# Decoder step on one core: nine more feed-forward slices as seven block products, and an activation table load given a fixed place

## The chip, the core and the metric

The kernel runs on 1 core of one Trainium2 chip. Its time is device time in microseconds, the median over runs. A core has five engines that run their own instruction queues and wait for each other by semaphores: TensorE (PE: matmuls, with weight loads shown apart as PEld), VectorE (DVE), ScalarE (ACT), GpSimd (POOL) and SyncE (SP, which here only issues DMAs). DMAs run on 16 engines that all queues share. Matmuls accumulate in PSUM, eight banks of 512 float32 a partition; all else lies in SBUF.

## The reference

A two-layer decoder step for 1024 prompt tokens and 8 sample tokens, model width 1024. Each layer has a mixer (layer 0: a gated recurrence, layer 1: stick-breaking attention; both in parallel with attention into 256 memory tokens) and a SwiGLU feed-forward network with inner width 2816. RMSNorm stands around every sub-layer. The part that the change touches is

```
def swiglu(h, w_gu, w_down):
    gate, up = jnp.split(h @ w_gu, 2, axis=-1)
    return (jax.nn.silu(gate) * up) @ w_down
...
    h = h + rmsnorm(swiglu(rmsnorm(h, g[2]), w_gu[l], w_down[l]), g[3])
```

with w_gu of 1024 x 5632 and w_down of 2816 x 1024 per layer.

## The kernel before, in words

Tokens are cut into two groups, g = 0 with 512 prompt tokens and g = 1 with 512 prompt and the 8 sample tokens (520 columns, handled as two halves of 260). Activations lie transposed, features on the partitions. A float32 product is made of three reduced-precision ones: activations and weights are split into a high and a low part (`split_to`, `split_w`), and high x high, high x low and low x high are summed in PSUM.

**Plain slices.** The feed-forward network is worked through in 22 slices of 128 inner columns, grouped into five parts (`PARTS`: 5, 5, 4, 4 and 4 slices). For each slice `ffn.part` makes gate and up with `proj` (line 269), each 8 blocks x 3 products x 2 halves, so 96 matmuls of 260 columns for g = 1; the gate goes through `silu` (Exp, Ln, Exp on ACT), and the product is split for the down projection. After a part's slices come 8 down columns, added into the float32 result R by DVE. A slice of weights is four loads of 256 KB (`split_w`): SP issues the load into a `wraw` tile, ACT copies the high part to a `wspl` tile, DVE subtracts for the low part. PSUM is a pool `mmp` of two double banks, a pool `smp` of three and one of one bank.

**Block-product slices.** Layer 1's second group is computed last, by `ffn_w`. There the gate/up product of a slice is seen as a 2 x 2 by 2 x 2 block product and made from seven block products (`gate_up_w`, line 526) of 4 x 3 = 12 matmuls each, 84 in all. The operands are sums of weight blocks and sums of activation blocks. The weight sums lie in DRAM: `weight_sums` (line 590) issues eight DMAs for each part on POOL's queue, half of them copies and half of them accumulating into their target, each behind a mark that POOL executes when a given value is there. In the kernel before, ACT copies that value into a small tile first (line 604). The activation sums are made by `sums_w` (line 329) on DVE and ACT during the first, plain slices (`gate_up_q`, which uses ACT's Silu instead of Exp, Ln, Exp). A block slice loads seven pieces of 256 KB, four of them from the sums.

The block slices use four PSUM tiles q0 to q3 (`Q`), in a pool `quads` with two buffers of each, opened after `mmp`, `smp` and `nsp` are closed (lines 1441 and 1442). Within a slice the tiles are chained: pb starts as -pa (L561), pc as -pb (L564), pd is copied out (L570), and L572 to L578 form gate times up.

**Order.** The program is traced in the order that `weave` gives: it takes steps from several generators in proportion to the weights written beside them. A scheduler then places each engine's instructions by that order and by its own costs, taking one that is ready ahead of one that is not. `tc.issue_after(ins)` ties the instructions of its block that run on the engine of `ins` behind `ins`; on other engines it orders nothing. The stage with layer 0's second group reads

```
    weave((chain(b0.sb(), b0.mem()), 30), (chain(f1.part(0), f1.part(1)), 18), (islice(ws, 16), 17))
    weave((chain(f1.part(2), f1.part(3), f1.part(4)), 24), (ws, 24))
```

where `ws` are the weight sums for layer 1: 16 of them beside parts 0 and 1, 24 beside parts 2 to 4. In the last stage `ffn_w(1, o1.x, 4)` has four plain slices and 18 block slices. Its end, `finish_rows` (line 749), sums squares on PE, takes Ln and Exp on ACT and forms the output rows on DVE. `nc.scalar.preload_act_table_set` (line 661) names the table set that holds both Ln and Exp; it has no operand, so nothing but the trace order places it.

## Time and profile before

| | |
|---|---|
| median of 3 runs | 2532.29 us (2530.27 to 2533.87) |
| the profiled execution | 2531.92 us, span 2530.2 us |
| TensorE clock granted, mean | 0.997 |
| matmuls | 15437 |
| block slices: matmuls under L554 | 864 + 648 |
| HBM read and written | 325.73 and 75.94 MB |

The span runs from the first to the last instruction on the core. A row of the timeline gives start, length, engine, line, operation, output and input tiles, shape and count; neighbours of one kind are merged, and the bracket names the idle time before and what ended it. A row of waits gives the waiting instruction, what released it, the total, the number of times and the longest. A row of stretches gives the stretch, its length, busy time and number of instructions of PE, PEld, DVE, ACT and POOL, then the granted clock, the share of time in which the 16 DMA engines worked, and GB/s. A queue's row gives packets, MB and the share of 16 engines' time; a DMA group's row the number of transfers, their size and the median time from issue to landing.

### The profile page before, as it was taken

Reading aid. Unit: us, or ns where it says so; the run is one execution under the profiler, and the core shown is the slowest. Engines: PE = TensorE matmul, PEld = TensorE weight load, DVE = VectorE, ACT = ScalarE, POOL = GpSimd, SP = SyncE. Lnnn points to the kernel's source line nnn. Section 1 sums busy time; section 2 is a strip of 40 time slices with the busy share of each in tenths; the row PEclk is TensorE's granted clock in tenths of the full one; section 3 lists DMA queues with packets and bytes.
Section 4 is the critical chain, followed back from the end, with each engine's and each line's share of the span. In section 5 each row is a group of like instructions: output and inputs, shape, how many; then the busy total and the mean of one; then the engine's idle time right before and its main releaser. Section 6 shows DMA issues by size and latency. Waiting matters only on the chain. (4 is left out here: it accounts for less than half of the span.)

```text
span 2530.2 us, 40541 instructions
## 1 busy us (share of the span) xinstructions
PE 2499.1 (99%) x15437; PEld 2169.2 (86%) x15437; DVE 1572.9 (62%) x2811; ACT 1199.7 (47%) x2294; POOL 91.5 (4%) x139
## 2 busy tenths in 40 slices
PE   8999999999999999999999999999999999999998
PEld 6888888877877888999999989876676797999997
DVE  6666556654765576655444585667577648855665
ACT  6346543243433454555333454555454445554444
POOL 1000000000000000000111100011000000000000
PEclk9999999999999999999999999999999999999998
DMA  6352242233644446476778866444343334365542
GB/s 186 111 163 67 71 154 80 63 107 117 180 125 129 129 146 190 145 179 168 182 198 212 245 186 191 152 147 118 112 146 117 97 114 122 121 188 145 150 139 68
DMA packets 502221, 358.20 MB, mean 142 GB/s; under 512 B 19077, under 2 KB 451794, under 8 KB 502026
## 3 DMA queue, kind: packets, MB, share of 16 engines
q1 hardware_dynamic: 483466, 301.08, 39.8%
q0 software_dynamic: 18560, 54.53, 8.9%
q8 instruction: 121, 1.98, 0.3%
q14 instruction: 74, 0.61, 0.1%
HBM read 325.73 MB, written 75.94 MB: 159 GB/s over the span
## 5 line engine op out<-in xcount | busy, mean ns | idle before, releaser
L277 PE MATMUL mm<-x,ws 128*128 128x260 f32 (+1 forms) x7968 | 1421.9, 334 | 0.8 <-ACT x L401 0.8
L277 PEld LDWEIGHTS mm<-x,ws 128*128 128x128 f32 x7968 | 1191.1, 188 | 173.4 <-issue 23.5
L263 ACT CAST ws<-w 128x512 fp32r<-128x512 f32 x728 | 430.7, 592 | 747.3 <-PE mm L277 610.5
L264 DVE TENSOR_TENSOR ws<-w,ws 128x512 fp32r<-128x512 f32 x728 | 474.3, 655 | 310.7 <-ACT ws L263 294.4
L277 PE MATMUL mm<-m,ws 128*128 128x512 f32 (+1 forms) x2112 | 414.3, 347 | 0.0
L277 PEld LDWEIGHTS mm<-m,ws 128*128 128x128 f32 x2112 | 325.8, 188 | 54.6 <-issue 9.5
L669 PE MATMUL q<-m,ws 128*128 128x260 f32 x1056 | 128.8, 283 | 0.0
L669 PEld LDWEIGHTS q<-m,ws 128*128 128x128 f32 x1056 | 127.2, 188 | 0.4 <-ACT hT L487 0.2
L545 DVE TENSOR_TENSOR ws<-w,ws 128x512 fp32r<-128x512 f32 x126 | 86.5, 691 | 59.9 <-ACT ws L544 56.2
L554 PE MATMUL q<-y,ws 128*128 128x260 f32 x864 | 113.0, 283 | 0.0
L544 ACT CAST ws<-w 128x512 fp32r<-128x512 f32 x126 | 77.9, 621 | 67.7 <-PE q L669 26.9
L294 DVE TENSOR_SCALAR t<-mm 128x512 f32<-128x512 f32 (+1 forms) x82 | 56.8, 693 | 82.6 <-PE mm L277 82.3
L554 PEld LDWEIGHTS q<-y,ws 128*128 128x128 f32 x864 | 107.6, 188 | 0.0
L449 DVE TENSOR_TENSOR r<-r,mm 128x512 f32<-128x512 f32 (+1 forms) x96 | 66.1, 689 | 62.4 <-PE mm L277 61.5
L705 DVE TENSOR_TENSOR t<-t,mm 128x512 f32<-128x512 f32 (+1 forms) x66 | 45.6, 690 | 85.9 <-PE mm L277 85.9
L298 DVE TENSOR_TENSOR t<-t,t 128x512 f32<-128x512 f32 (+1 forms) x66 | 45.8, 694 | 68.1 <-ACT t L297 68.1
L554 PE MATMUL q<-x,ws 128*128 128x260 f32 x648 | 86.3, 282 | 0.0
L554 PEld LDWEIGHTS q<-x,ws 128*128 128x128 f32 x648 | 81.3, 188 | 0.0
L317 DVE TENSOR_TENSOR st<-st,n 128x512 f32<-128x512 f32 (+1 forms) x98 | 67.3, 694 | 6.6 <-ACT n L316 5.0
L285 DVE TENSOR_TENSOR m<-t,m 128x512 fp32r<-128x512 f32 (+1 forms) x88 | 61.0, 693 | 2.5 <-ACT m L284 1.4
L284 ACT CAST m<-t 128x512 fp32r<-128x512 f32 (+1 forms) x88 | 54.9, 624 | 12.7 <-DVE t L705 2.5
L1135 PEld LDWEIGHTS s<-a,a 128*128 128x128 f32 x448 | 53.4, 192 | 1.2
(334 smaller groups left out, 2466.2 us busy)
## 6 DMA issues: line engine op xcount, KB each, us to landing
w<-in_w_gu SPq DMA_DIRECT2D x334, 256.0 KB, 3.3
w<-in_w_down SPq DMA_DIRECT2D x160, 256.0 KB, 2.8
w<-in_w_in_a SPq DMA_DIRECT2D x80, 256.0 KB, 2.9
wsum<-in_w_gu POOLq DMA_DIRECT2D x18, 1024.0 KB, 9.0
w<-wsum SPq DMA_DIRECT2D x72, 256.0 KB, 3.4
w<-in_w_o SPq DMA_DIRECT2D x64, 256.0 KB, 2.9
wsum<-in_w_gu POOLq DMA_DIRECT2D x12, 1280.0 KB, 10.1
w<-in_w_mem_kv SPq DMA_DIRECT2D x32, 256.0 KB, 2.9
```

The lines of the kernel that those rows point to most:

```text
L263: nc.scalar.copy(ws[:, 0, :n, :], raw[:, :n, :])
L264: nc.vector.tensor_sub(ws[:, 1, :n, :], raw[:, :n, :], ws[:, 0, :n, :].bitcast(F32))
L277: nc.tensor.matmul(ps[:, a, : PW[g]], wt, xt[k][:, xi, o : o + PW[g]], start=(k == 0 and wi == 0), stop=(k == nk - 1 and wi == 2),)
L284: nc.scalar.copy(dst[0], src)
L285: nc.vector.tensor_sub(dst[1], src, dst[0].bitcast(F32))
L294: nc.vector.tensor_scalar(sv(x, g), pv(ps, g), -44.0, None, op0=ALU.max)
L317: nc.vector.tensor_add(acc[:, :n], acc[:, :n], t[:, :n])
L449: nc.vector.tensor_add(dst, dst, pv(ps, g))
L544: nc.scalar.copy(w[:, 0, :], src)
L545: nc.vector.tensor_sub(w[:, 1, :], src, w[:, 0, :].bitcast(F32))
L554: nc.tensor.matmul(ps[:, :h], w[:, wj, k * P : (k + 1) * P], x[:, xi, :], start=(first and k == 0 and wi == 0), stop=(k == 3 and wi == 2), ...
L669: nc.tensor.matmul(pp[a][:, :h], wt, mids[k][:, xi, a * h : (a + 1) * h], start=(k == 0 and wi == 0), stop=(k == nf - 1 and wi == 2),)
```

## The change

Three things are edited together.

1. Parts 2 to 4 of layer 0's second group go from `ffn` to `ffn_w`. Slices 10 to 12 are plain (`gate_up_q`) and make the activation sums on the way, slices 13 to 21 are block slices. Their weight sums are 24 further DMAs on POOL's queue, woven into layer 0's first half. `ffn_w` takes the lists of steps, the first part and R as arguments; outside the last stage its extra buffers come from other pools. The last stage gets three plain slices instead of four.
2. PSUM: `smp` and `nsp` stay open throughout; `set_banks` exchanges only `mmp` for `quads`, which now has one buffer of each of four tiles. The exchange happens three times instead of once. `S()` and `NS()` use their own banks in the last stage too.
3. Small ties: POOL's mark reads the value itself instead of ACT's copy of it; the activation sums are spread over the matmuls of the plain slices, tied to a matmul instead of a DVE multiplication; the table preload is tied behind the last Silu.

```diff
+    def set_banks(one):
+        nonlocal mmp
+        banks.close()
+        single.clear()
+        if one:
+            single.append(banks.enter_context(tc.tile_pool(name=nm("quads"), bufs=1, space=PSUM)))
+        else:
+            mmp = banks.enter_context(tc.tile_pool(name=nm("mmp"), bufs=2, space=PSUM))
...
-    def gate_up_q(l, f, xt):
+    def gate_up_q(l, f, xt, side, n_side):
...
-                        nc.tensor.matmul(
+                        ins = nc.tensor.matmul(
...
+                c = j * ND + k + 1
+                for _ in range(c * n_side // 16 - (c - 1) * n_side // 16):
+                    with tc.issue_after(ins.ins):
+                        next(side, None)
...
-                    nc.scalar.activation(d, pp[a][:, :h], AF.Silu)
+                    act[0] = nc.scalar.activation(d, pp[a][:, :h], AF.Silu)
...
-                tok = small([P, 1], tag="rr")
-                nc.scalar.copy(tok, after())
-                mark = nc.gpsimd.tensor_copy(small([P, 1], tag="mk", bufs=1), tok)
+                mark = nc.gpsimd.tensor_copy(small([P, 1], tag="mk", bufs=1), now[0])
...
-        def __init__(self, l, x, plain):
-            self.g, self.l, self.x, self.ops, self.plain, self.n, self.r, self.pi = 1, l, x, [], plain, 0, 0, 0
+        def __init__(self, l, x, steps, first, rows, R=None):
+            self.g, self.l, self.x, self.ops, self.steps, self.rows = 1, l, x, [], steps, rows
+            self.first, self.plain, self.n, self.r, self.pi = first, PARTS[first][0] + len(steps), 0, 0, 0
...
-            if self.pi and self.n % 8 in (1, 4, 6):
+            if (self.pi or not self.rows) and self.n % 8 in (1, 4, 6):
                 return cpool.tile([P, 2, 512], F32R, tag="c", name=nm("ws"))
...
-            if self.pi and self.r % 2:
+            if not self.rows and self.r % 2:
+                return B().rearrange("p (k m) -> p k m", k=4)
+            if self.rows and self.pi and self.r % 2:
...
-                nc.scalar.preload_act_table_set("natural_log_exp_and_others")
+                with tc.issue_after(act[0].ins):
+                    nc.scalar.preload_act_table_set("natural_log_exp_and_others")
...
+    w0 = weight_sums(0, range(2, 5))
-    weave((a0.mem(), 8), (a1.fq(), 8))
+    weave((a0.mem(), 8), (a1.fq(), 8), (islice(w0, 6), 7))
...
-    weave((o0.finish(), 17), (chain(a1.v(), a1.qm(A)), 8))
+    weave((o0.finish(), 17), (chain(a1.v(), a1.qm(A)), 8), (islice(w0, 6), 7))
...
-    weave((a1.core(), 22), (f0.part(0), 9))
+    weave((a1.core(), 22), (f0.part(0), 9), (islice(w0, 8), 9))
...
-    weave((a1.sample(), 6), (a1.gate(), 4), (f0.part(1), 9))
+    weave((a1.sample(), 6), (a1.gate(), 4), (f0.part(1), 9), (w0, 5))
...
-    weave((chain(f1.part(2), f1.part(3), f1.part(4)), 24), (ws, 24))
+    set_banks(True)
+    fw = ffn_w(0, o1.x, (5, 6, 5), 2, False, f1.R)
+    weave((chain(fw.part(2), fw.part(3), fw.part(4)), 24), (ws, 24))
+    f1.acc = fw.acc
+    set_banks(False)
...
-    banks.close()
-    single.append(ctx.enter_context(tc.tile_pool(name="quads", bufs=2, space=PSUM)))
-    f1 = ffn_w(1, o1.x, 4)
+    set_banks(True)
+    f1 = ffn_w(1, o1.x, (5, 6, 5), 0, True)
```

More of the change, by code (lines that the diff above doesn't have):

```diff
@@ L114, in S @@
     def S():
-        if single:
-            turn[0] += 1
-            return Q(3 * (turn[0] % 2))
         return smp.tile([P, 512], F32, tag="s", name=nm("s"))
@@ L575, in gate_up_w @@
         product(pb, 6)
-        nc.scalar.activation(sg[:, h:n], gt[:, :h], AF.Silu)
+        act[0] = nc.scalar.activation(sg[:, h:n], gt[:, :h], AF.Silu)
         nc.vector.tensor_mul(sg[:, :h], sg[:, :h], pb[:, :h])
@@ L580, in gate_up_w @@
         split_to((mt[:, 0, :n], mt[:, 1, :n]), sg[:, :n])
+        now[0] = mt[:, 0, 0:1].bitcast(F32)
         return mt
+    now = [None]
+    act = [None]
     sums = {}
@@ L648, in part @@
                 if f0 + j < self.plain:
-                    mt, ins = gate_up_q(l, f0 + j, self.x)
-                    mids.append(mt)
-                    with tc.issue_after(ins.ins):
-                        for _ in range((1, 2, 1, 0)[j]):
-                            next(self.sums, None)
+                    mids.append(gate_up_q(l, f0 + j, self.x, self.sums, self.steps[j]))
+                    now[0] = mids[-1][:, 0, 0:1].bitcast(F32)
                 else:
@@ L678, in part @@
                         nc.vector.tensor_add(d, d, pp[a][:, :h])
+                now[0] = self.R[m][:, 0:1]
                 if last:
                     sq_acc(self.acc, self.R[m][:, :n], m, n)
+                if last and self.rows:
                     nc.scalar.activation(self.R[m][:, :n], self.R[m][:, :n], AF.Copy, scale=gcol(l, 3, m))
@@ L1002, in heads2 @@
             evac(out[-1][:, h % 2, :], ps, g)
+            now[0] = out[-1][:, h % 2, 0:1]
             yield
```

52 lines of the change are left out of this document (26 added, 26 removed).

## The prediction

> **What bounds the kernel now.** I read the page's head first, then the list of what TensorE (PE) waits for, then PE's timeline in the two stretches that the change touches, the end of the kernel, and last the DMA queues of the first stretch.
>
> ```profile
> span 2530.2 us, 40541 instructions
> PE 2499.1 (99%) x15437; PEld 2169.2 (86%) x15437; DVE 1572.9 (62%) x2811; ACT 1199.7 (47%) x2294; POOL 91.5 (4%) x139
> ...
> PE s L177 <- DMA prow<-in_hg_norm: 5.3, 1, 5.3
> ...
> PE q L771 <- DVE yT L775: 1.8, 1, 1.8
> PE q L512 <- DVE r L449: 1.7, 1, 1.7
> ```
>
> PE is busy for 2499.1 of 2530.2 us, and its largest waits lie at the start and the end. So time is gained by taking matmuls away, provided that everything behind them keeps pace, or by shortening the end. PE's timeline prices the matmuls:
>
> ```profile
> 1253.52 46.07 PE L277 MATMUL mm<-x,ws 128*128 128x260 f32 x384
> 1299.43 23.20 PE L277 MATMUL mm<-m,ws 128*128 128x260 f32 x192
> ...
> 2384.19 1.60 PE L554 MATMUL q<-x,ws 128*128 128x260 f32 x12
> 2394.29 1.60 PE L554 MATMUL q<-x,ws 128*128 128x260 f32 x12
> ```
>
> The first row is four plain gate/up slices of layer 0, 96 matmuls each. Start to start it is 1299.43 - 1253.52 = 45.91 us, 11.48 us a slice. The last two rows are the first products of two neighbouring block-product slices of layer 1: 2394.29 - 2384.19 = 10.10 us for 84 matmuls. PE waits in neither stretch.
>
> **The matmuls removed.** Nine slices of layer 0 (13 to 21) change form. The diff also sets the last stage's first block-product slice from 4 to 3 (three plain slices instead of four), so a tenth follows. Gain: 10 x (11.48 - 10.10) = 13.8 us, all of it on PE's path if nothing else comes late.
>
> **The table load at the end.** The rows of ScalarE's (ACT's) table loads and the end of the timeline:
>
> ```profile
> L134 ACT ACT_TABLE_LOAD x1 | 1.3, 1283 | 0.8 <-PEq L1466 0.8
> L519 ACT ACT_TABLE_LOAD x1 | 1.3, 1283 | 0.0
> L758 ACT ACT_TABLE_LOAD x1 | 1.3, 1283 | 1.4 <-PE q L756 1.4
> L759 ACT ACT_TABLE_LOAD x1 | 1.3, 1283 | 0.0
> ...
> 2517.46 1.28 ACT L758 ACT_TABLE_LOAD   x1 [1.43 <-PE q L756]
> 2518.92 0.24 ACT L761 ACTIVATE rr<-q,epsb 8x1 f32<-8x1 f32 x1
> 2519.17 1.28 ACT L759 ACT_TABLE_LOAD   x1
> 2520.70 0.75 DVE L772 SCALAR_TENSOR_TENSOR yT<-yT,rr,hT 128x512 f32<-128x512 f32 x1 [4.70 <-ACT rr L759]
> ```
>
> L661's preload has no row: it was placed ahead of the Silu load of L519, where the old set was still in, and did nothing. Hence two loads stand between the last sums and the output rows, and VectorE (DVE) waits for them. Tied behind the last Silu, the preload runs during the last down products, and both loads go: 2 x 1.28 = 2.5 us (rounded down). What is late next is the Ln/Exp pair itself. Layer 0 gets a Silu load and a preload of its own, 1.28 us each; ACT is under half busy and nothing ends on it there, so nothing. [...]
>
> **PSUM.** Double-buffered banks become four single ones. The tightest handover is pb, read by L577 and overwritten by the next slice's L561:
>
> ```profile
> 2457.69 1.59 PE L554 MATMUL q<-x,ws 128*128 128x260 f32 x12
> 2458.04 0.42 DVE L577 TENSOR_TENSOR t<-t,q 128x260 f32<-128x260 f32 x1
> 2459.32 0.37 ACT L561 ACTIVATE q<-q 128x260 f32<-128x260 f32 x1 [0.20 <-PE q L554]
> ...
> 2125.00 21.14 PE L277 MATMUL mm<-m,ws 128*128 128x512 f32 x90
> 2147.05 0.69 DVE L449 TENSOR_TENSOR r<-r,mm 128x512 f32<-128x512 f32 x1
> 2147.89 2.02 PE L512 MATMUL q<-x,ws 128*128 128x260 f32 x15 [1.75 <-DVE r L449]
> ```
>
> L577 ends at 2458.46, L561 starts at 2459.32: 0.86 us to spare, so one buffer costs nothing between slices. At a change of pools PE waits for the last evacuation, 1.75 us here. There will be two more such changes, each between 0 (the first tile falls on the bank freed earlier) and 1.75 us: 0 to 3.5, I take 1.75.
>
> **DVE before the first block slice of the last stage.** It now has three plain slices, not four, to make the activation sums:
>
> ```profile
> 2148.00:2190.00 42.00, 42.00 (x347) 41.52 (x348) 41.97 (x93) 22.06 (x47) 0.00 (x0) 1.00 0.29 82
> ...
> 2161.51 1.11 DVE L343 TENSOR_TENSOR b<-x 128x260 f32<-128x260 f32 x3
> 2189.92 0.44 DVE L285 TENSOR_TENSOR y<-b,y 128x260 fp32r<-128x260 f32 x1
> ```
>
> DVE (third busy column) is full, 41.97 of 42 us, and the sums end at 2190.36; PE will want them from about 2147.9 + 3 x 11.48 = 2182.3 on, or 5 us behind that for the last ones, as the products take them in turn. But the sums are no longer held behind the slice's own multiplication (the tie names a matmul, which orders nothing on DVE), so they can start ahead of 2161.51, and the finish of the other half can go behind them. Bounds 0 to 8 us; I take 0, being nearest to a reordering. In layer 0 no such neighbour competes: 0.
>
> **The early weight sums.** 24 more sums are issued by GpSimd (POOL), woven from a0's memory attention to the sampling stage. POOL's mark now reads the activation itself, so a later writer of it could wait for POOL; the next write is a part away (45.9 + 23.2 us by the first two timeline rows). Rows of three stretches, the DMA share next to last:
>
> ```profile
> 344.00:391.00 47.00, 46.98 (x376) 44.86 (x377) 35.75 (x60) 25.08 (x46) 0.00 (x0) 1.00 0.46 141
> 528.00:652.00 124.00, 124.00 (x621) 96.73 (x620) 69.25 (x112) 48.02 (x84) 0.00 (x0) 0.99 0.42 122
> 1043.00:1235.00 192.00, 191.69 (x1388) 177.47 (x1387) 107.09 (x216) 101.20 (x223) 20.41 (x33) 1.00 0.66 168
> ```
>
> The third already carries sums beside plain projections at a share of 0.66, and PE loses 0.3 us. The early ones start from 0.46 and less, so 0 to 3 us, taken as 0.
>
> **DMA in layer 0's block slices, the large unknown.** A block slice loads 7 x 256 KB where a plain one loads 4, and in this stretch POOL's sums for layer 1 are in flight. Queues q0 (sums) and q1 (weights), with median landing times, of the whole stretch, of 4 us in which a sum runs, and of block slices without sums:
>
> ```profile
> q0 software_dynamic: 9461, 24.92, 47.4%
> q1 hardware_dynamic: 42092, 23.27, 35.7%
> ...
> w<-in_w_gu SPq DMA_DIRECT2D x41, 256.0 KB, 5.3
> ```
>
> ```profile
> q0 software_dynamic: 316, 0.65, 99.5%
> ...
> w<-in_w_gu SPq DMA_DIRECT2D x2, 256.0 KB, 7.3
> ```
>
> ```profile
> q1 hardware_dynamic: 12772, 6.34, 54.2%
> ...
> w<-wsum SPq DMA_DIRECT2D x10, 256.0 KB, 3.6
> ```
>
> ```profile
> ACT ws L263 <- DMA w<-in_w_gu: 4.5, 3, 4.0
> ```
>
> In 1255 to 1480 us the queues take 47.4 + 35.7 = 83.1% of 225 us, 187.0 us of work. q1 moved 23.27 MB in 80.3 us, so 256 KB take 0.90 us. The change adds 9 x 3 loads: 24.4 us, together 211.4 us, to a stretch that shrinks by 9 x 1.38 to 212.6 us. That is a share of 0.99. From 1318 to 1322 us q1 moves no packet at all while a sum runs, and a load lands after 7.3 instead of 3.6 us; such loads leave ACT waiting, 4.0 us once in the plain kernel. ACT's split copies then hold up L561 and L564 behind them, on which PE waits within 1.4 us. If the engines can be kept full, the cost is 0. If they sustain only the 88% that they reached over 35 us (56.4% + 31.6%, next row), the stretch takes 211.4 / 0.88 = 240.2 us and the cost is 27.6 us.
>
> ```profile
> q0 software_dynamic: 1722, 4.44, 56.4%
> q1 hardware_dynamic: 6363, 3.16, 31.6%
> ```
>
> Against that: those 35 us had spare demand, not a ceiling; loads are prefetched into ten raw and some eight split tiles (about 18 x 1.44 = 26 us of PE work), and POOL's sums may run late, as nothing reads them before the last stage (2148 us). I take 6 us, a ceiling near 97%, nearer to the zero end.
>
> [...]
>
> **The sum.** -13.8 - 2.5 + 1.75 + 6 = -8.5 us. The profiled execution took 2531.92 us with its span of 2530.2, and the median is 2532.29, so 0.4 more: 2532.3 - 8.5 = 2523.8, called 2524.
>
> **The rivals.** (1) The sums leave the weights their share, DMA costs nothing: 2532.3 - 14.5 = 2518, and 2516 if the pool changes cost nothing. For it: no PE wait in the present stretch, deep prefetch. (2) Starvation eats the gain: at a ceiling of 93.5% the term is 13.5 us, 2531. For it: the share of 0.99. (3) Slower: the same mechanism at the 88% ceiling, 27.6 us, gives 2532.3 - 14.5 + 27.6 = 2545. It decides from a term of 14.5 + 5.1 = 19.6 us, a ceiling of 91%. (4) DVE's sums come late in the last stage, 5 us: 2529. (5) The tie doesn't bring the load ahead of the last Ln: 2526.5, still faster.
>
> **How the numbers follow.** A measurement here can tell about 0.2%, 5.1 us, from no change. Forecast 0.38, with (5) inside it, from 2518 to 2527; rival 1 has 0.20; rival 2 0.21 and rival 4 0.04, both mostly within 0.2%; rival 3 0.17. So faster 0.58, same 0.25, slower 0.17. The range runs from rival 1's better end, less 2 us of scatter, to the middle of rival 3: 2514 to 2540; the forecast's own is 2518 to 2527.
>
> **What would show it.** Block slices between 1270 and 1440 us 10.1 us apart, with gaps in PE only where a sum with accumulation is in flight; ACT's wait on DMA for weights growing from 4.5 us to tens if rival 2 or 3 holds; q0 and q1 near 99% there. Table loads under L519 twice and the preload's line twice, none under L758 and L759. A PE gap at each pool change. PE's first block product in the last stage at about 2182 minus what was gained before. A shortfall with DMA well under 90% would make my reason wrong.

## The result, and the profile after

The changed kernel takes 2543.03 us (median, 2541.03 to 2545.00); the kernel before takes 2532.29 us beside it. The ratio is 1.0038, with a 95% interval of 1.0027 to 1.0049: slower by 10.7 us, where 8.5 us less were forecast. The profiled execution took 2543.03 us with a span of 2541.3 us. The head of its page, and the largest waits of TensorE (PE) in it:

```profile
span 2541.3 us, 40618 instructions
PE 2497.6 (98%) x15317; PEld 2162.3 (85%) x15317; DVE 1598.9 (63%) x2920; ACT 1211.3 (48%) x2320; POOL 116.4 (5%) x187
```

```profile
PE q L682 <- DVE r L691: 7.2, 6, 3.1
PE q L513 <- DVE r L450: 5.5, 2, 4.0
...
PE mm L281 <- DVE r L691: 0.9, 1, 0.9
```

120 matmuls are gone (15437 to 15317), as the change says. Yet PE is busy only 1.5 us less, and it idles 43.7 us in place of 31.1. Both halves want an explanation: new waits, and matmuls that became slower. (Line numbers have moved: L277 is now L281, L512 is L513, L554 is L559, the down columns of the block form are L682 and their addition into R is L691.)

**Where it happened.** The stretch from layer 0's first plain slice of the second half to its last down column, as one window row of the changed kernel, and, in the kernel before, the row of PE's timeline that follows the stretch which began at 1253.52 us:

```profile
1261.15:1469.88 208.73, 201.57 (x1620) 199.14 (x1620) 113.67 (x214) 89.70 (x173) 35.84 (x53) 0.98 0.97 253
```

```profile
1460.39 5.70 PE L277 MATMUL mm<-x,ws 128*128 128x512 f32 x24
```

Before: 1460.39 - 1253.52 = 206.87 us. After: 208.73 us, with 9 x 12 matmuls fewer. PE was busy for 201.57 us of it, at a granted clock of 0.98 (the column behind the fifth engine), and the DMA share, next to last, was 0.97. Stage by stage, each boundary read from PE's timelines:

| stretch | before | after | difference | forecast |
|---|---|---|---|---|
| start to the pool change | to 1253.52 | to 1257.16 | +3.6 | 0 |
| two pool changes (waits of PE) | 0 | 3.99 + 0.90 | +4.9 | +1.75 |
| layer 0's second half | 206.87 | 208.73 | +1.9 | -12.4 + 6 |
| up to the last stage | 687.50 | 688.39 | +0.9 | 0 |
| last stage, first slice to last down column | 366.03 | 368.25 | +2.2 | -1.4 |
| from there to the end | 16.28 | 13.88 | -2.4 | -2.5 |

**How a gap comes about.** The longest gap in the down columns, on all engines (timeline of the changed kernel; start, duration, and in brackets the idle time before and what ended it):

```profile
1449.58 0.76 DVE L691 TENSOR_TENSOR r<-r,q 128x260 f32<-128x260 f32 x2 [0.16 <-PE q L682]
1456.00 0.62 ACT L267 CAST ws<-w 128x512 fp32r<-128x512 f32 x1 [7.38 <-DMA w<-in_w_down]
1456.52 0.63 ACT L320 ACTIVATE n<-r 128x520 f32<-128x520 f32 x1
1456.65 0.69 DVE L268 TENSOR_TENSOR ws<-w,ws 128x512 fp32r<-128x512 f32 x1 [6.31 <-ACT ws L267]
1457.26 0.69 DVE L321 TENSOR_TENSOR st<-st,n 128x520 f32<-128x520 f32 x1
1457.87 0.75 DVE L691 TENSOR_TENSOR r<-r,q 128x260 f32<-128x260 f32 x2
1458.43 1.98 PE L682 MATMUL q<-m,ws 128*128 128x260 f32 x8 [3.07 <-DVE r L691]
```

Read it upwards from the last row. PE stood 3.07 us for VectorE's (DVE's) addition of the column two before, which frees a PSUM tile (the down columns take two pairs of tiles in turn). That addition had not been waiting for PE: it stood behind L268 in DVE's order, the second half of the split of a later weight tile, which waited 6.31 us for its first half on ScalarE (ACT), which waited 7.38 us for a weight load. PE did not lack the late tile itself, which belongs to the last column, two further on; it lacked the PSUM that an engine held up by that tile was to free. PE's six waits on L691, 7.2 us in the list above, all lie in these down columns; inside layer 0's block slices it has none.

**What follows a gap.** Steps of 3.41 us of the changed kernel, about three places where PE stood:

```profile
1257.49:1260.91 3.42, 0.00 (x0) 0.00 (x0) 2.90 (x7) 2.41 (x5) 0.00 (x0) 1.00 0.49 134
1260.91:1264.32 3.41, 3.17 (x14) 3.20 (x15) 2.91 (x7) 0.93 (x2) 0.00 (x0) 0.50 1.04 299
1264.32:1267.73 3.41, 3.41 (x30) 3.41 (x30) 2.19 (x6) 1.95 (x4) 0.00 (x0) 1.00 0.86 230
...
1318.94:1322.35 3.41, 1.65 (x12) 1.46 (x12) 1.97 (x4) 1.14 (x2) 0.00 (x0) 1.00 0.97 342
1322.35:1325.76 3.41, 3.19 (x16) 2.92 (x14) 1.91 (x5) 1.98 (x4) 0.15 (x1) 0.50 0.41 116
...
1383.79:1387.21 3.42, 2.30 (x17) 2.15 (x18) 2.68 (x7) 0.00 (x0) 0.84 (x2) 1.00 1.12 286
```

In the steps behind the first two places the granted clock is 0.50: 14 matmuls in 3.41 us where the next step does 30. So each of these gaps cost its own length and about 1.7 us more, half of 3.41, which the profile books as busy time. Behind the third, where PE was busy for 2.30 of 3.42 us, the granted clock stayed at 1.00. The changed kernel has six such halved steps ahead of its end (from 585.1, 612.4, 1260.9, 1322.4, 1458.9 and 1721.7 us), the kernel before has one (608.8). Five more are some 8.5 us, and they are the greater part of why PE's busy time fell by 1.5 us and not by the 13.8 that the removed matmuls were to bring.

### The profile page after: what moved, and what is told of

The parts are those of the page before. It is cut to its first block, busy times and chain, and to the rows that moved or that the text cites. A ratio compares the mean times of both kernels' runs of the same rounds, so it can differ in the third digit from the quotient of the medians.

```text
span 2541.3 us, 40618 instructions
## 1 busy us (share of the span) xinstructions
PE 2497.6 (98%) x15317; PEld 2162.3 (85%) x15317; DVE 1598.9 (63%) x2920; ACT 1211.3 (48%) x2320; POOL 116.4 (5%) x187
## 5 line engine op out<-in xcount | busy, mean ns | idle before, releaser
L281 PE MATMUL mm<-x,ws 128*128 128x260 f32 (+1 forms) x6816 | 1284.5, 344 | 3.6 <-ACT x L402 1.4
L281 PEld LDWEIGHTS mm<-x,ws 128*128 128x128 f32 x6816 | 1053.8, 189 | 176.6 <-issue 25.3
L267 ACT CAST ws<-w 128x512 fp32r<-128x512 f32 (+1 forms) x688 | 405.5, 590 | 644.9 <-PE mm L281 488.5
L268 DVE TENSOR_TENSOR ws<-w,ws 128x512 fp32r<-128x512 f32 (+1 forms) x688 | 446.0, 652 | 312.7 <-ACT ws L267 295.8
L281 PE MATMUL mm<-m,ws 128*128 128x512 f32 (+1 forms) x1536 | 346.1, 372 | 0.0
L281 PEld LDWEIGHTS mm<-m,ws 128*128 128x128 f32 x1536 | 257.5, 189 | 54.8 <-issue 9.5
L682 PE MATMUL q<-m,ws 128*128 128x260 f32 x1632 | 205.1, 286 | 7.2 <-DVE r L691 7.2
L682 PEld LDWEIGHTS q<-m,ws 128*128 128x128 f32 x1632 | 200.2, 191 | 10.0 <-issue 4.3
L550 DVE TENSOR_TENSOR ws<-w,ws 128x512 fp32r<-128x512 f32 x164 | 112.4, 691 | 85.5 <-ACT ws L549 83.4
L549 ACT CAST ws<-w 128x512 fp32r<-128x512 f32 x164 | 101.4, 620 | 105.6 <-PE q L682 30.2
L559 PE MATMUL q<-x,ws 128*128 128x260 f32 x1008 | 134.4, 283 | 0.0
L559 PEld LDWEIGHTS q<-x,ws 128*128 128x128 f32 x1008 | 126.5, 188 | 0.0
L559 PE MATMUL q<-y,ws 128*128 128x260 f32 x912 | 119.5, 284 | 0.2 <-ACT q L566 0.2
L559 PEld LDWEIGHTS q<-y,ws 128*128 128x128 f32 x912 | 113.6, 189 | 0.6 <-ACT q L566 0.4
L298 DVE TENSOR_SCALAR t<-mm 128x512 f32<-128x512 f32 (+1 forms) x70 | 48.4, 691 | 62.8 <-PE mm L281 62.4
L513 PE MATMUL q<-x,ws 128*128 128x260 f32 x576 | 72.8, 288 | 6.5 <-DVE r L450 5.5
L513 PEld LDWEIGHTS q<-x,ws 128*128 128x128 f32 x576 | 71.0, 192 | 8.3 <-ACT a L288 4.2
L691 DVE TENSOR_TENSOR r<-r,q 128x260 f32<-128x260 f32 x112 | 42.5, 421 | 37.9 <-PE q L682 37.9
```

The source lines that it names most:

```text
L267: nc.scalar.copy(ws[:, 0, :n, :], raw[:, :n, :])
L268: nc.vector.tensor_sub(ws[:, 1, :n, :], raw[:, :n, :], ws[:, 0, :n, :].bitcast(F32))
L281: nc.tensor.matmul(ps[:, a, : PW[g]], wt, xt[k][:, xi, o : o + PW[g]], start=(k == 0 and wi == 0), stop=(k == nk - 1 and wi == 2),)
L298: nc.vector.tensor_scalar(sv(x, g), pv(ps, g), -44.0, None, op0=ALU.max)
L513: ins = nc.tensor.matmul(pp[a][:, :h], wt, xt[k][:, xi, a * h : (a + 1) * h], start=(k == 0 and wi == 0), stop=(k == ND - 1 and wi == 2),)
L549: nc.scalar.copy(w[:, 0, :], src)
```

## The experiments

The theory at this point: layer 1's last 24 weight sums, moved by GpSimd's (POOL's) DMA, run beside layer 0's block slices and delay their weight loads; the late tile blocks ACT and then DVE, PSUM is freed late, PE stands, and the clock is halved behind it. The rivals: the single PSUM buffers and the pool changes cost this by themselves; the loss lies in the early sums of layer 0; it lies in the last stage with its three plain slices. Ratios are to the kernel before, measured beside each.

| kernel | what differs | median, us | ratio (95% interval) | layer 0's second half, us |
|---|---|---|---|---|
| before | | 2532.29 | | 206.87 |
| changed | | 2543.03 | 1.0038 (1.0027 to 1.0049) | 208.73 |
| E_plain0 | layer 0's nine slices plain, its banks as before | 2534.00 | 1.0009 (1.0000 to 1.0018) | 207.02 |
| G_banks_plain | nine slices plain, new banks kept | 2540.86 | 1.0029 (1.0020 to 1.0038) | 208.60 |
| M_no_sums | 24 sums left out | 2528.53 | 0.9977 (0.9968 to 0.9987) | 196.36 |
| A_sums_later | 24 sums in the next attention | 2561.13 | 1.0101 (1.0087 to 1.0116) | 196.29 |
| H_sums_early | all 40 sums earlier | 2553.62 | 1.0075 (1.0061 to 1.0089) | 194.78 |
| I_spread | sums in four other places | 2563.00 | 1.0126 (1.0108 to 1.0145) | 194.88 |
| K_pace | 16 sums before the pool change faster | 2549.35 | 1.0065 (1.0051 to 1.0080) | 213.16 |
| L_beside | 12 sums beside slices, 12 elsewhere | 2534.88 | 1.0004 (0.9994 to 1.0013) | 196.67 |
| N_first | as L, the other 12 at the start | 2563.70 | 1.0124 (1.0107 to 1.0141) | 198.28 |
| B_last_four | four plain slices in the last stage | 2543.80 | 1.0044 (1.0027 to 1.0061) | 209.47 |
| C_both | A and B | 2561.84 | 1.0112 (1.0097 to 1.0126) | 196.13 |
| D_tie | before, with only the table load tied | 2531.33 | 0.9987 (0.9978 to 0.9996) | |

### Is it layer 0's stage at all?

E puts the nine slices back into the plain form and the double-buffered banks, and keeps all else.

```diff
-    set_banks(True)
-    fw = ffn_w(0, o1.x, (5, 6, 5), 2, False, f1.R)
-    weave((chain(fw.part(2), fw.part(3), fw.part(4)), 24), (ws, 24))
-    f1.acc = fw.acc
-    set_banks(False)
+    weave((chain(f1.part(2), f1.part(3), f1.part(4)), 24), (ws, 24))
```

> The changed kernel with layer 0's slices 10 to 21 plain again, in the double-buffered PSUM of before: no block slice of layer 0 and no pool change about them, the 24 weight sums of layer 1 beside the plain slices as in the kernel before. What is left of the change: layer 0's early sums (made, but not used), the last stage's three plain slices, the table load behind the last Silu. First theory (the whole loss sits in the stage of the block slices): the time is that of the kernel before, plus up to 3.5 us for the early stage, plus 1.7 for the last, minus 2.4 for the tail: 2531 to 2535. Rival (early sums and last stage cost more than the markers show): 2538 to 2542.

Measured: 2534.00 us, ratio 1.0009 (1.0000 to 1.0018), inside the first theory's range. So what is left of the change (early sums, last stage, tail) together costs between nothing and 0.18%; the greater part of the 0.38% needs the nine block slices or what was built around them.

### Banks and pool changes, or block slices beside sums?

G keeps the new banks, the pool changes and the sums, and makes all twelve slices plain.

```diff
-    fw = ffn_w(0, o1.x, (5, 6, 5), 2, False, f1.R)
+    fw = ffn_w(0, o1.x, (0,) * 12, 2, False, f1.R)
```

> The changed kernel with its pool changes and its single-buffered PSUM tiles kept in that stage, and the 24 sums of layer 1 beside it, but with all twelve slices plain, so that each slice loads 16 weight tiles of 128 KB a row block less than the block form does and reads no summed tile. First theory (block slices and sums together ask for more than the queues give): the gaps of 1.76, 1.16 and 3.07 us in the down columns go, what stays is the pool changes, at 1 to 4 us each with the halved clock behind them: 2534 to 2539. Rival (one buffer per PSUM tile makes TensorE stand in the down columns): the gaps of over 1 us in the down columns stay and nine slices are 12.4 us dearer as well: 2550 to 2556.

(The expectation's count of weight tiles is muddled: a plain slice loads 4 x 256 KB and a block slice 7.) Measured: 2540.86 us, 2 us over the first theory's range. PE's waits in 1250 to 1480 us, all of them, and the stage's row:

```profile
PE q L513 <- DVE r L450: 4.0, 1, 4.0
PE mm L281 <- DVE r L691: 0.9, 1, 0.9
```

```profile
1258.61:1467.21 208.60, 208.60 (x1728) 208.39 (x1728) 88.56 (x161) 65.32 (x116) 27.88 (x45) 0.99 0.82 209
```

No gap is left in the down columns: 208.60 us busy of 208.60, and without the one halved step behind the pool change (1.7 us) that is 206.9, the pace of the kernel before. So one buffer per PSUM tile cost nothing with plain slices, even with the sums running. (No run has block slices beside the sums with two buffers for each tile, so whether a second one would have hidden the late additions is not known.) The pool change, however, costs its 4.0 us here too, plus the halved step, plus 0.9 at the change back: 6.6 us, not 1.75.

### Taking the sums out of the stage

M leaves the 24 sums out; the last stage does the same work on layer 0's sums in their place.

```diff
-    ws = weight_sums(1, range(5))
+    ws = weight_sums(1, range(2))
...
-    weave((chain(fw.part(2), fw.part(3), fw.part(4)), 24), (ws, 24))
+    drain(fw.part(2), fw.part(3), fw.part(4))
+    for i in (2, 3, 4):
+        sums[1][i] = sums[0][i]
```

> The changed kernel without layer 1's last 24 weight sums: they are made nowhere, and the last stage's block slices of parts 2 to 4 read the sums of layer 0 in their place, tile for tile of the same size (so this part of the result is not the reference's; the work of TensorE, VectorE and ScalarE is the same). It prices the 24 sums alone, with no other place to bear them. First theory: the down columns lose their gaps, the stage of the block slices ends some 17 us earlier against the changed kernel (it ended 10 us ahead of the kernel before's pace in the kernels that had the sums elsewhere, and 7 behind it in the changed one), the pool change at 1256 us stays at about 4 us because the 16 sums ahead of it stay: about 14 us under the changed kernel, 2527 to 2531. Rival (the moved sums had cost something in that stage too, or block slices cost more by themselves): 2535 to 2543.

Measured: 2528.53 us, inside the first theory's range and faster than the kernel before. The stage's row:

```profile
1258.26:1454.62 196.36, 196.36 (x1620) 195.73 (x1620) 115.19 (x214) 90.82 (x173) 7.97 (x8) 0.99 0.53 155
```

Busy without a break: 208.73 - 196.36 = 12.4 us were the sums' price. Of these 7.2 us are PE's gaps and some 3.4 two halved steps behind them (the one behind the pool change is in M's row too); the other 1.8 us are busy time that these rows do not explain. ScalarE's waits for weights show the sums as well. The changed kernel between 1255 and 1480 us:

```profile
ACT ws L549 <- DMA w<-wsum: 13.7, 3, 5.6
...
ACT ws L267 <- DMA w<-in_w_down: 9.5, 2, 7.4
```

In M the first of these is 4.6 us between 1262 and 1470 us, and there is none for the down projection's tiles. The DMA views of the stage, first of the changed kernel, then of M, then of G (queue, packets, MB, share; and median landing time of the down projection's tiles):

```profile
q0 software_dynamic: 9440, 25.17, 49.7%
q1 hardware_dynamic: 51632, 27.49, 46.6%
...
w<-in_w_down SPq DMA_DIRECT2D x24, 256.0 KB, 8.0
```

```profile
q1 hardware_dynamic: 52896, 28.11, 49.0%
...
w<-in_w_down SPq DMA_DIRECT2D x24, 256.0 KB, 2.8
```

```profile
q0 software_dynamic: 8554, 22.60, 46.7%
q1 hardware_dynamic: 38110, 20.77, 34.5%
...
w<-in_w_down SPq DMA_DIRECT2D x24, 256.0 KB, 7.9
```

The sums take a tile's landing from 2.8 to 8.0 us. In G it is 7.9 us as well, with no gap. So late landing alone did no harm there; it did with block slices, which draw 7 tiles in 10.06 us through the same prefetch instead of 4 in 11.48 us. That the prefetch is what runs dry there is argued from these rows, not shown.

### Elsewhere with the sums

A moves the 24 sums into the attention stage that follows.

```diff
-    weave((chain(fw.part(2), fw.part(3), fw.part(4)), 24), (ws, 24))
+    drain(fw.part(2), fw.part(3), fw.part(4))
...
-        (chain(f0.part(0), f0.part(1), f0.part(2), f0.part(3)), 34),
+        (chain(f0.part(0), f0.part(1), f0.part(2), f0.part(3)), 34), (ws, 27),
```

> The changed kernel, but the last 24 of layer 1's weight sums no longer run beside layer 0's block slices: they run beside group 1's attention of layer 1, the stage after. First theory (the sums' transfers hold back the weight tiles of the block slices; the late tile holds ScalarE and VectorE, PSUM is freed late, TensorE stands still and its granted clock is halved for 3.4 us after each stand): ScalarE's waits on weight loads in this stage go from 5.1 to 7.4 us each to under 1 us, TensorE's gaps of 3.99, 1.76, 1.16 and 3.07 us between 1257 and 1456 us go but for a pool change of 1 to 2 us, the stage comes 14 to 19 us sooner, and the time is 2524 to 2529, if the attention stage bears the sums for nothing (up to 5 us more if not). Rival (one PSUM buffer per tile and the pool changes with their Silu are what makes TensorE stand): the gaps stay where they are and the time is 2541 to 2546. Rival (the cost lies in the early sums and in the last stage): this moves nothing either, 2541 to 2546.

```profile
1259.15:1455.44 196.29, 196.28 (x1620) 195.66 (x1620) 115.34 (x214) 90.78 (x173) 7.98 (x8) 0.99 0.52 155
```

The stage did as the first theory said, 196.29 us. The time did not: 2561.13 us, because the attention bore the sums far worse than the 5 us allowed. Two of its waits in 1480 to 2160 us, which the kernel before does not have among its largest:

```profile
DVE c L938 <- DMA b<-qd: 33.9, 10, 6.9
...
PEld s L1323 <- ACT b L288: 25.3, 22, 7.2
```

H makes all 40 sums earlier: 20 beside group 0's memory attention, 8 beside the part after it, 12 in the first half of the attention ahead of the pool change.

```diff
+    ws = weight_sums(1, range(5))
+    weave(
+        (chain(a1.merge(), a1.mem()), 12), (a1.mem_sample(), 20), (chain(f0.part(2), f0.part(3)), 16),
+        (islice(ws, 20), 20),
+    )
+    weave((f0.part(4), 8), (islice(ws, 8), 8))
...
-    weave((chain(b0.sb(), b0.mem()), 30), (chain(f1.part(0), f1.part(1)), 18), (islice(ws, 16), 17))
+    weave((chain(b0.sb(), b0.mem()), 30), (chain(f1.part(0), f1.part(1)), 18), (ws, 24))
```

> The changed kernel with layer 1's 40 weight sums made earlier: 20 beside the memory attention of group 0 and 8 beside the feed-forward part that follows (680 to 980 us, where the trace shows DMA shares of 0.39 to 0.56 and no work on GpSimd), 12 in the first half of the last attention of group 0; none runs beside the block slices of layer 0, none just before the pool change. First theory: no gap in the down columns, the pool change at about 1.75 us and not 4.0, since the 16 sums that ended there are gone too; the nine block slices then bring their 12.4 us, less 1.75 for each of the two pool changes, 1.7 for the last stage and up to 3.5 early, plus 2.4 in the tail: 2522 to 2527, faster than both kernels. Rival (sums cost the same wherever they run): 2538 to 2546. Rival (the pool change costs 4 us by itself): the gap at 1256 stays at 4 us, 2526 to 2530.

```profile
1289.71:1484.49 194.78, 194.78 (x1620) 194.15 (x1620) 115.11 (x214) 90.80 (x173) 7.97 (x8) 1.00 0.54 157
```

```profile
PE q L513 <- ACT a L288: 1.1, 1, 1.1
PE mm L281 <- DVE r L691: 0.8, 1, 0.8
```

The stage is at its best here: 194.78 us, no halved step, the pool change at 1.1 us. 206.87 - 194.78 = 12.1 us is what nine block slices bring, against the 12.4 of the forecast. But the time is 2553.62 us: my reading of idle queues between 680 and 980 us as free room was wrong. In 600 to 1260 us DVE waited for the caches' loads, and in 690 to 830 us PE waited in the memory attention:

```profile
DVE c L950 <- DMA c<-in_cache_mem_v: 30.9, 5, 11.7
```

```profile
PE s L904 <- DVE b L897: 8.4, 3, 4.6
PE mm L281 <- DVE r L450: 5.1, 3, 2.8
```

I avoids that stage and the block slices both, and lets the marks of the output projections' stage wait for its own rows (`now[0] = self.R[m][:, 0:1]` in `mm`). The 16 sums in the attention between run denser too (weight 24 in place of 17).

```diff
-    drain(f0.part(4))
+    weave((f0.part(4), 8), (islice(ws, 8), 8))
-    weave((f0.finish(True), 9), (o1.mm(a1.xo, 1, 5), 4))
-    weave((normed(0, f0.R, f0.r, gkvcol, xk0, True), 8), (o1.mm(a1.xo, 5, 7), 2))
+    weave((f0.finish(True), 9), (o1.mm(a1.xo, 1, 5), 4), (islice(ws, 5), 4))
+    weave((normed(0, f0.R, f0.r, gkvcol, xk0, True), 8), (o1.mm(a1.xo, 5, 7), 2), (islice(ws, 3), 2))
...
-    weave((f1.finish(True), 9), (o0.mm(b0.xo, 1, 5), 4))
-    weave((normed(1, f1.R, f1.r, gkvcol, xk1, True), 8), (o0.mm(b0.xo, 5, 7), 2))
+    weave((f1.finish(True), 9), (o0.mm(b0.xo, 1, 5), 4), (islice(ws, 5), 4))
+    weave((normed(1, f1.R, f1.r, gkvcol, xk1, True), 8), (o0.mm(b0.xo, 5, 7), 2), (ws, 2))
```

> The changed kernel with layer 1's 40 weight sums where the traces show neither block slices nor loads of caches: 8 beside the last part of layer 0's feed-forward of group 0 (in the kernel with the early sums that stretch, 830 to 900 us, had a DMA share of 1.00 and TensorE busy 70.00 of 70 us), 8 beside layer 1's output projection of group 0, 16 in the first two thirds of the attention that follows, 8 beside layer 0's output projection of group 1. First theory: the down columns of the block slices keep pace, the pool change costs about 1.1 us as in that kernel, and the nine block slices show: the stage 5 to 8 us shorter than in the kernel before, the tail 2.4 us shorter, the last stage 1.7 longer: 2523 to 2530. Rival (each place that takes sums loses as much as the block slices did): 2536 to 2545.

A miss: 2563.00 us. The block slices took 194.88 us again, so that half holds, but the output projections were the worst place yet:

```profile
900.00:1000.00 100.00, 82.27 (x452) 69.28 (x452) 52.38 (x83) 36.71 (x65) 17.97 (x17) 0.90 0.93 242
```

In the changed kernel PE is busy for 99.97 us of the same hundred. The rival of this run, that every place which takes sums loses as much as the block slices did, was too mild.

### The pool change

K alters one number, so that the 16 sums ahead of the pool change end earlier.

```diff
-    weave((chain(b0.sb(), b0.mem()), 30), (chain(f1.part(0), f1.part(1)), 18), (islice(ws, 16), 17))
+    weave((chain(b0.sb(), b0.mem()), 30), (chain(f1.part(0), f1.part(1)), 18), (islice(ws, 16), 26))
```

> The changed kernel with one number altered: the 16 sums beside the last attention of group 0 are issued faster (weight 26 in place of 17 in the interleaving), so that they end some 80 us before the pool change and not at it; the 24 beside the block slices stay. If the gap of 3.99 us at the first pool change comes of sums still running there: it falls to 1.1 to 1.75 us, the halved clock behind it may stay, the down columns keep their gaps: 2539 to 2541. If it is the price of the pool change: no difference, 2543.

All of PE's waits between 1100 and 1300 us:

```profile
PE s L1335 <- DVE b L1288: 4.0, 1, 4.0
PE s L1323 <- DVE b L1328: 2.3, 1, 2.3
PE q L513 <- ACT a L288: 1.1, 1, 1.1
PE s L1323 <- ACT b L288: 0.5, 1, 0.5
```

The gap at the pool change fell from 3.99 to 1.1 us, as in H and I, where the sums had also ended before (the stage behind it in H has a granted clock of 1.00): 2.9 us of it were the sums', and 1.1 us are the change's own. With the 0.8 us at the change back (H) that is 1.9 us, about the 1.75 that the forecast has for both. The time was a miss, 2549.35 us: the denser sums opened two gaps of 2.3 and 4.0 us in the attention, at 1139.6 and 1144.4 us, and behind them matmuls of 260 columns took 0.24 to 0.25 us each (8 in 1.94 us, 14 in 3.48 us) where the ten ahead of the gaps had taken 0.14 (1.36 us). (The stage behind took 213.16 us, 4.4 more than in the changed kernel: PE's gaps in it add up to 11.3 us in place of 7.2. Why they are longer is open.)

### How many sums the block slices bear

L lets 12 sums run there, each beside a slice and not beside down columns.

```diff
-    weave((chain(fw.part(2), fw.part(3), fw.part(4)), 24), (ws, 24))
+    for pi in (2, 3, 4):
+        for j, _ in enumerate(fw.part(pi)):
+            if j < 3:
+                drain(islice(ws, (2, 1, 1)[j]))
+    drain(ws)
...
-    weave((a1.sample(), 6), (a1.gate(), 4), (f0.part(1), 9), (w0, 5))
+    weave((a1.sample(), 6), (a1.gate(), 4), (f0.part(1), 9), (chain(w0, islice(ws, 4)), 9))
-    drain(f0.part(4))
+    weave((f0.part(4), 8), (islice(ws, 8), 8))
```

> The changed kernel with the 24 sums thinned out where the block slices run: 12 of them, each issued so that it runs beside a gate-and-up slice and not beside down columns (2, 1 and 1 behind the first three slices of each part); of the others 8 beside the last part of layer 0's feed-forward of group 0, which bore 8 with at most one gap of 0.97 us in two kernels, and 4 beside part 1 of it; 16 ahead of the pool change as in the changed kernel. First theory (the block slices bear a running sum at 10.06 us each, the down columns do not): the gaps in the down columns go or halve, the stage gains 9 to 14 us over the changed kernel, the moved sums cost up to 3 us: 2530 to 2537. Rival (a sum costs its 0.7 us wherever in this stage it runs, and about 1 us outside): 2540 to 2546.

```profile
1264.75:1461.42 196.67, 195.32 (x1620) 194.25 (x1620) 113.96 (x214) 89.99 (x173) 25.49 (x32) 1.00 0.81 219
```

2534.88 us, as the first theory had it, and level with the kernel before. The stage took 196.67 us, 1.9 over H, with one gap of 1.3 us and no halved step. So 12 sums cost 1.9 us there (3.5 in N, which has the same 12 there) and 24 cost 12 to 14: the price is not one of so much for each sum. Halving their number and keeping them off the down columns came together in this kernel; which of the two did it isn't told apart. The other 12 were dearer than the 3 us that I allowed. The sums of squares on PE (L310, L306 in the kernel before) come at the same places of each program and serve as markers: by them L is 9.0 us behind the kernel before at 914 us. Of these 2.0 us are there at 198 us, ahead of any sum, 3.2 come until 626 us (3.0 in the changed kernel, which lacks these sums) and 3.8 beside the 8 sums after that.

N moves those 12 to the start.

```diff
+    ws = weight_sums(1, range(5))
...
         (chain(mem_load(), mem_keys(0), mem_values(0), mem_keys(1), mem_values(1), a0.qm(M)), 22),
+        (islice(ws, 12), 14),
```

> The kernel with 12 sums beside the slices of layer 0, with one thing altered: its other 12 run beside the first core of group 0's mixer and the projections of the memory keys and values (60 to 230 us, DMA share 0.25 to 0.60 in the changed kernel), and not beside parts 1 and 4 of layer 0's feed-forward, where they had cost 4 to 7 us by the markers. First theory (a sum is free where TensorE's weight loads leave the queues half idle): the early markers stay within 1.5 us of the kernel before, the stage of the slices is as in the kernel with 12, the time 2528 to 2532, at or under the kernel before with the table load tied (2531.3). Rival (a sum costs about half a microsecond or more in any stage that is bound by TensorE): 2534 to 2542.

A plain miss: 2563.70 us. PE's largest wait in 60 to 250 us and the one behind it:

```profile
PE mm L837 <- ACT t L834: 16.2, 3, 8.6
```

```profile
DVE t L839 <- DMA mks<-t: 24.5, 4, 10.9
```

Twelve sums cost some 33 us here: DVE waited up to 10.9 us until a store of the memory keys had left its tile. ACT's copy L834 takes tiles that such stores leave too; PE's longest wait, 8.6 us, is for a copy that itself waited 9.70 us for a store. A stage with DMA shares of 0.25 to 0.60 was not room.

### The last stage and the tail

B gives the last stage its fourth plain slice back, C joins that with A.

```diff
-    f1 = ffn_w(1, o1.x, (5, 6, 5), 0, True)
+    f1 = ffn_w(1, o1.x, (4, 4, 4, 4), 0, True)
```

> The changed kernel with four plain slices ahead of the last feed-forward's block slices instead of three (layer 1's last stage as many as before, four sums to each slice). Theory of the last stage (three slices give VectorE too little time for the 16 sums' products, so the first block slices stand): the last stage gives back its 1.7 us of loss against the kernel before or less, less the 1.4 us that the tenth block slice saves: 2540 to 2544, about 2542. If the last stage were the seat of the whole loss: 2532 to 2536. If VectorE's load there is harmless: 1.4 us slower than the changed kernel, 2544.4.

> Both edits: the 24 weight sums beside the attention that follows, and four plain slices in the last stage. First theory: the gain of the sums' move and that of the last stage add up, 2523 to 2529. Rival of the PSUM buffers: 2540 to 2544, as with the four slices alone.

B takes 2543.80 us and C 2561.84, no different from the changed kernel and from A; C's expectation fell with A's. B's time lies inside its first theory's range and 0.6 us from the 2544.4 of the other, so it does not decide between them. Its stage in layer 0 repeats what the changed kernel shows: 9.1 us of gaps, all in the down columns and all behind L691. The last stage of the kernel before, of the changed kernel and of B:

```profile
2147.89:2513.92 366.03, 366.02 (x3048) 364.53 (x3049) 226.13 (x438) 189.81 (x386) 0.00 (x0) 1.00 0.46 135
```

```profile
2159.17:2527.42 368.25, 366.92 (x3036) 363.37 (x3037) 228.33 (x442) 193.90 (x394) 0.00 (x0) 1.00 0.48 137
```

```profile
2154.62:2522.72 368.10, 367.45 (x3048) 364.49 (x3049) 226.65 (x438) 191.69 (x387) 0.00 (x0) 1.00 0.47 135
```

With the same 3048 matmuls B needs 2.1 us more than the kernel before: what is left between the two there is one buffer per PSUM tile in place of two, and the order in which activation sums are woven in. The tenth block slice takes 12 matmuls away (3036), and the stage is still no shorter than B's. So this term is two: 2.1 us for the new banks or order, and a saving of 1.4 us that three plain slices do not deliver. Each is read from one trace of a kernel.

D is the kernel before with the table load alone tied.

```diff
-                    nc.scalar.activation(d, pp[a][:, :h], AF.Silu)
+                    act[0] = nc.scalar.activation(d, pp[a][:, :h], AF.Silu)
...
-        nc.scalar.activation(sg[:, h:n], gt[:, :h], AF.Silu)
+        act[0] = nc.scalar.activation(sg[:, h:n], gt[:, :h], AF.Silu)
...
-                nc.scalar.preload_act_table_set("natural_log_exp_and_others")
+                with tc.issue_after(act[0].ins):
+                    nc.scalar.preload_act_table_set("natural_log_exp_and_others")
```

> The kernel before with nothing changed but ScalarE's table load issued behind the last Silu. By the rows of the two traces two of the tail's loads of 1.23 to 1.28 us go: 2529.8, that is 2.5 us under the kernel before, 2.4 by the tail of the changed kernel's trace. If the tail's loads lie beside other work: 2532.3, no difference.

2531.33 us, ratio 0.9987 (0.9978 to 0.9996), by its interval 1 to 5.6 us faster: the only kernel with the whole computation that beats both. Its stretch from the last down column to the end is 2529.8 - 2516.34 = 13.46 us, 2.8 us less than the 16.28 before.

## Why the prediction was wrong, point by point

The first step that failed is the wait that it gave the late weight tiles: they were to hold up ACT's L561 and L564 inside the block slices, and the cost was sized at 6 us from the queues' share. In layer 0's block slices PE has no such wait; it stood in the down columns, behind DVE's additions, and the sums cost 12.4 us. The second is the price of the pool changes, taken from one without a sum beside it: 1.75 us forecast, 6.6 measured. The third is that a stand of PE was given no price beyond its own length, where a halved step behind it adds some 1.7 us. The differences from the forecast are 6.4 us for the sums, 4.9 for the pool changes, 3.6 for the last stage, 3.6 at the start and 0.9 in between; they make up the 19.6 us from the forecast of -8.5 to the +11.1 of the spans but for 0.2 us.

**The matmuls removed: right for nine, wrong for the tenth.** Forecast 10 x 1.38 us. Nine slices bring 12.1 us where nothing disturbs them (H), and they ran about 10.06 us apart in the changed kernel too. The tenth brought nothing that shows: the last stage takes 368.25 us with it and 368.10 without (B).

**The table load: right.** The Ln and Exp of the end (L758 and L759 before) load no table any more; the Silu's line and the preload's (L519 and L661 before, now L524 and L674) do so twice each:

```profile
L524 ACT ACT_TABLE_LOAD x2 | 2.6, 1283 | 0.0
L674 ACT ACT_TABLE_LOAD x2 | 2.6, 1283 | 0.0
L138 ACT ACT_TABLE_LOAD x1 | 1.3, 1283 | 0.8 <-PEq L1486 0.8
```

The tail is 2.4 us shorter (2.8 in D), for 2.5 forecast.

**DMA in layer 0's block slices: the mechanism was named, the term was too small.** Forecast +6 of a range of 0 to 27.6; measured 12.4 (the changed kernel against M). The share of the two queues was 49.7 + 46.6 = 96.3% of the stage, near the ceiling of 97% that I took, but the ceiling was the wrong measure. I let the queues' work set the stage's length. What set it was how late single tiles came at the down columns, and who stood behind the engine that waited. I had followed a late tile through ACT's order to L561 and L564, which write the slice's PSUM tiles, and not through DVE's order to the PSUM tile that DVE was to free in a down column. The signs named for a slower outcome came: ACT's waits for weights grew to tens of us, and the two queues reached 96.3%. With both queues asked for much, landing went from 2.8 to 8.0 us.

**The pool changes: out of their bounds.** Forecast 1.75, bounds 0 to 3.5; measured 3.99 + 0.90 and a halved step of 1.7, together 6.6 us. The changes themselves are 1.1 and 0.8 us (H, I, K), as forecast; the rest, 2.9 us of waiting and the halved step behind it, came of the 16 sums still running there. I priced it from a pool change that had no sum beside it (2146 us) and took that for its upper end.

**PSUM between slices: right in layer 0** (H and M: no gap in three plain slices, nine block slices and 24 down columns without sums; G: none with sums and plain slices). In the last stage up to 2.1 us are unexplained, and the new banks are one of two candidates.

**DVE before the first block slice of the last stage: named, taken as 0.** Against the forecast the last stage is 3.6 us worse, inside its bounds of 0 to 8. PE did wait there for a split, 0.76 us at 2173.5 us, with DVE busy for 39.56 of the 40 us from 2159.2 on.

**The early sums: 3.6 us by the table, bound 3; not all theirs.** In E, G, M and B, which have the same early sums, the kernel stands only about 0.6 to 1.2 us behind the kernel before at 626 us, and nearly all of that is there at 198 us already, while the first of these sums is issued at 301 us; D, which has none, stands 2.1 us behind. In the changed kernel 3.0 of the 3.6 us come between 527 and 626 us: PE has one gap of 1.2 us there, behind DVE's L298, and two halved steps (585 and 612 us) where the kernel before has one. Such a gap, of 1.2 to 2.1 us, is in eight of the twelve kernels with these sums (not in A, E, G and M), and neither in the kernel before nor in D. So the sums cost 0 to 2 us there; halved steps whose cause is open (last section) come on top.

**What had no term at all: the clock.** Five halved steps more, 1.7 us each, are 8.5 of the 19 us between forecast and time (they lie inside the terms above). Three lie in layer 0's second half: one behind the pool change, which M has too, and two behind gaps of the down columns, 3.4 of the 12.4 us. The others lie at 585 and 1721 us. This is the step that was missing: every wait of PE was priced at its own length.

Of the rivals, the slower one (the sums starve the weights, deciding from a term of 19.6 us) had the right cause, but its own term reached only 12.4, nearer to the 13.5 of rival (2), which was to end at 2531; with the pool changes at 6.6, the last stage at +2.2 and 3.6 at the start the sign changed all the same. I had valued the terms one by one, though two of them hang on the same sums.

## What to carry to other kernels

An engine's order is part of the price of a late load: ask what stands behind the instruction that waits for it, above all whether that frees a PSUM tile. The 24 sums in the background cost PE nothing beside the plain form of this stage (busy for 220.00 of 220 us in the kernel before) and 12.4 us beside the leaner block form, so that nine block slices that gain 12.1 us lost it all; before moving such transfers elsewhere, look at which stores and loads of that stage are waited for at once, since a DMA share of 0.25 to 0.60 there told nothing (12 sums cost 33 us in N). Price a gap on TensorE with the clock behind it: one of 1.76 us at 1319 us cost 3.5 us here, with its halved step.

## What the runs showed of the hardware

In the traces of the changed kernel and of the kernel before the granted clock is 1.00 or 0.50, and within each it changes on one grid of 3.41 us: the halved steps of the changed kernel at 1260.9, 1322.4, 1458.9 and 1721.7 us begin 18, 40 and 77 steps apart. Away from the start, the end and the stretch of 533 to 623 us, a step at 0.50 came in the changed kernel behind steps in which PE was busy for 0.00, 0.45, 1.38 and 1.65 us, and not behind one with 1.77 us (at 1783.2 us) or any with more. In the kernel before it came behind none, the lowest two having 1.66 us (2144.8 us) and 1.78 us (1707.9 us). A gap of 1.76 us inside one step was so followed by the half clock (changed kernel, 1319.0 us), and one of 1.75 us inside one step was not (before, 2146.1 us), nor one of 2.26 us that lay across two steps (before, 1709.6 us).

At the end of both the half clock came behind steps with more, 1.93 us before and 2.26 us after, and between 533 and 623 us behind steps with PE shown busy throughout (3.41 us: 15 and 13 matmuls in the changed kernel, 13 in the kernel before). So busy time as the profile has it is not all that counts; what else does, no run here tells.

By how far the markers of PE's timeline fell back, a weight sum cost some 1.0 us in H (28 us for 28), 1.3 to 1.5 in C and A (31 and 35 us for 24), 2.8 in N (33 us for 12) and about 3 in I's first output projection (some 25 us for 8). The 24 beside plain slices cost PE nothing in the kernel before, where it is busy for 220.00 of 220 us from 1250 us on at a DMA share of 0.84. The share that a stage has without the sums does not tell these apart (N's dear 12 ran where the changed kernel has 0.25 to 0.60); in H and N the waits shown are those of engines for loads and stores of their own stage, 11.7 and 10.9 us at the longest, and that they make up the whole price is not shown.
